# Second FFN of a decoder layer: units of mixed and plain chunks in turn, half-size raw buffers, output tiles turned over DRAM

## The chip, the cores and the metric

The kernel runs on one core of a Trainium2 chip. The metric is the device time of one execution in microseconds (us), as the median of several runs. The engines are TensorE (PE in the profile; its weight loads are PEld), VectorE (DVE), ScalarE (ACT), GpSimd (POOL) and SyncE (SP), which issues the weight transfers.

## What is computed

One layer of a decoder trunk on 256 positions (plus 16 meta tokens ahead of them), width 2048, in float32:

```
h = h + 0.5 * swiglu(rms_norm(h, g1), w_gate1, w_up1, w_down1)          # first FFN
z = rms_norm(h, g_mix) @ w_in                                           # attention, short convolution
h = h + (sigmoid(ga) * y_attn + sigmoid(gc) * y_conv) @ w_out           # output projection
h = h + 0.5 * swiglu(rms_norm(h, g2), w_gate2, w_up2, w_down2)          # second FFN, inner width 5632
return h[:, 16:]                                                        # the meta tokens are dropped

swiglu(x, g, u, d) = (silu(x @ g) * (x @ u)) @ d
```

The change lies in the second FFN and in the end of the output projection that feeds it. There the 256 positions are two tiles of 128 (j = 1, 2).

## The kernel before

**Numbers.** Each float32 operand is split into two float32r parts, `hi` and `lo`, and each product is three matmuls (`trio`, L360: x_hi w_hi, x_hi w_lo, x_lo w_hi). Activations are split once. Weights are split as they stream in: ScalarE copies the raw weight to `whi` (L129), VectorE subtracts to get `wlo` (L130).

**The stream of weights.** `Stream` (L71) is one list of raw loads and one list of *units*. A load is 2048 columns of 128 rows (1 MB), taken by SP into one of three buffers (`RAW_BUFS`). A unit is what is split at once, up to 1024 columns, two blocks of 512. `next` hands units to TensorE's code in order. When it turns to a unit it first runs the steps that are due in the queue `first` (put there by `early`), then splits the unit three ahead (`AHEAD`), then runs the due steps of the queue `waiting` (put there by `later`, with a lag in units; lag 1 is the very next unit). This fixes each engine's program order: all engines take their instructions in that order, and `split_pool` holds the parts of four units, so the split of a unit waits until TensorE has left the unit four earlier.

**Second FFN (`ffn_tokens`, L568).** The inner width is done in two groups of 6 and 5 *passes* (`GROUPS`). A pass (f) makes 512 gate columns and 512 up columns for both position tiles: 8 *chunks* of 256 input rows, each holding four 128 x 512 weight blocks. After the passes of a group come the down projections, in two halves (d = 0, 2) of two 512-column output tiles each, with 12 or 10 chunks.

A *plain* chunk is two units of four products: 8 products, 24 matmuls. A *mixed* chunk is a 2 x 2 x 2 block product by Strassen's method in Winograd's form: 7 products, 21 matmuls, in the four units a, b, c, d (2, 2, 2, 1 products). It asks VectorE for four sums of weight blocks (`part`, L138: t3 and b12 with a; t2 and t4 with b) and once per chunk place for sums of activations (`combos`, L585: four adds and a split into `comb` or `below`). In a pass the chunks `MIXED` (3 and 5) are mixed (in pass 0 of the first group only 5); in the down projections those in `DOWN_MIXED`.

**PSUM.** A pass uses all eight banks: four direct sums c[j, q] in the tiles `three` (two banks), `one` and `two`, and four sums m[1], m[5], m[6], m[7] of the mixed products in a second such set (`banks`, L667). The two sets change places from pass to pass: the next pass's direct sums go where this pass's mixed sums were, so these must be read out first. That is `spread` (L621): ScalarE copies m[1], then four VectorE adds combine m[6], m[7], m[5], m[5] into `u`. `gather` (L628) adds the direct sums and applies Silu on ScalarE, `times` (L636) multiplies gate and up.

**What follows a pass.** The product must be turned so that the inner dimension lies on the partitions. Between passes two large VectorE transposes of 32 x 32 blocks (`turn_blocks`, L643) are followed by five POOL transfers that move the blocks over DRAM (`move_blocks`, L652: one out, four back), and `split_blocks` splits into `mid`. After a group's last pass sixteen small transposes (`turn_columns`, L559) do it on VectorE alone. `down_combos` makes the activation sums of a mixed down chunk, 18 units after the pass that made its input.

**End of the output projection.** For each of four output tiles g, `add_out` (L1236) adds to the residual and sums squares, `turn_columns` turns the tile with sixteen small transposes between the next splits, and `to_act` (L1247) scales by the norm's gain and splits into `act`.

Of the kernel before, what the change touches and what calls it, by code (L numbers as in the profile page):

```python
# [65 lines left out]
MIXED = 3, 5  # L66
DOWN_MIXED = {6: (4, 6, 8), 5: (4, 7)}
RAW = 2048


class Stream:  # L71
# [14 lines left out]

    def add_mixed(self, src):

        g = len(self.loads)
        self.loads.append((src, RAW, ()))  # L90
        self.subs += [(g, part, 0, HALF) for part in "abcd"]

    def add(self, src, n, width, cuts=()):

        per = min(SUB // width, SUB // P)
        g = len(self.loads)
        self.loads.append((src, n * width, cuts))
        at = [0, *cuts, n] if cuts else [*range(0, n, per), n]
        for a, b in zip(at, at[1:]):
            self.subs.append((g, a * width, b - a, width))  # L100

    def load(self, upto, between=(), queues=()):
        between, queues = list(between), list(queues)
        while self.n_loaded < min(upto, len(self.loads)):
            src, n, cuts = self.loads[self.n_loaded]
            raw = self.raw_pool.tile([P, RAW], F32, name="raw")
            at = [0, *(c * P for c in cuts), n]
            for a, b in zip(at, at[1:]):
                (queues.pop(0) if queues else self.nc.sync).dma_start(raw[:, a:b], src[:, a:b])
                if between:  # L110
                    between.pop(0)()
            self.raw[self.n_loaded] = raw
            self.n_loaded += 1

    def split(self, upto):
        nc = self.nc
        while self.n_split < min(upto, len(self.subs)):
            g, c, kk, width = self.subs[self.n_split]
            self.load(g + RAW_BUFS)
            n = kk * width  # L120
            if n:
                raw = self.raw[g][:, c : c + n]
            else:
                raw = self.part(self.raw[g], c)
                n = raw.shape[1]
                kk = n // width
# [8 lines left out]
            if self.n_split == len(self.subs) or self.subs[self.n_split][0] > g or c == "b":  # L135
                self.load(g + 1 + RAW_BUFS)

    def part(self, raw, name):  # L138

        sub, add = self.nc.vector.tensor_sub, self.nc.vector.tensor_add  # L140
        b11, b12, b22, b21 = (raw[:, i * HALF : (i + 1) * HALF] for i in range(4))
        t3, t2, t4 = (self.mix[:, i * HALF : (i + 1) * HALF] for i in range(3))
        if name == "a":
            sub(t3, b22, b12)
            sub(b12, b12, b11)
            return raw[:, 2 * HALF :]
        if name == "b":
            add(t2, t3, b11)
            sub(t4, b21, t2)
            return raw[:, : 2 * HALF]  # L150
# [40 lines left out]
def tile_decoder_layer(  # L191
# [50 lines left out]
    gu = down = 0  # L242
    for n in GROUPS:
        for i in range(gu, gu + 8 * n):
            if i % 8 in MIXED[i < 8 :]:
                st.add_mixed(wgu2[i])
            else:
                st.add(wgu2[i], 4, 512)
        for pair in range(2):
            for i in range(2 * n):  # L250
                if i in DOWN_MIXED[n]:
                    st.add_mixed(wd2[down])
                else:
                    st.add(wd2[down], 4, 512)
                down += 1
        gu += 8 * n
# [9 lines left out]
    ssq = [const.tile([P, T], F32, name=f"ssq{i}") for i in range(2)]  # L266
    R = const.tile([P, T], F32, name="R")
    R2 = const.tile([P, T], F32, name="R2")
# [96 lines left out]
    def quads(c, m, x, mixed, n, after_mixed, tail=False):  # L365
# [4 lines left out]
        plan = []  # L370
        for i in range(n):
            k = 2 * i
            if i in mixed:
                s = [None, *(lambda part, q=q, i=i: mixed[i](q, part) for q in range(4))]
                plan.append([
                    [(c[1, 1], s[4], 0), (c[1, 0], of(k + 1, 1), 1)],
                    [(m[1], of(k, 1), 0), (m[5], s[1], 1)],
                    [(m[7], s[3], 0), (m[6], s[2], 1)],
# [13 lines left out]
        for i, units in enumerate(plan):  # L392
# [6 lines left out]
            if i == max(mixed):  # L399
                after_mixed()  # L400
# [998 lines left out]
```

## Time and profile before

| | us |
|---|---|
| median of 3 runs (2130.96 to 2131.1) | 2131.1 |
| the profiled execution, its own time | 2130.72 |
| its span, first to last instruction | 2129.0 |
| first matmul of the second FFN, from the span's start | 1419.12 |
| last matmul | 2124.10 |
| TensorE busy | 2118.0 (99%) |
| VectorE busy | 1489.5 (70%) |
| ScalarE busy | 1015.7 (48%) |
| granted TensorE clock, mean over the span | 1.0 of full speed |

A row of the timeline gives start (us from the span's start), length (us), engine, line, operation, output<-input and, behind x, how many like it follow each other; in square brackets stands how long the engine was idle ahead of it and what ended that. Matmuls are pipelined: their shown lengths (0.39 us) overlap, so it is the distance between starts that tells whether TensorE was held up. Rows of the order, in fences of their own, show in which order an engine's instructions stand; they hold no times.

### The profile page before, as it was taken

What the parts mean: (1) busy time and instruction counts of PE and PEld (TensorE: products, weight loads), DVE (VectorE), ACT (ScalarE), POOL (GpSimd) and SP (SyncE); (2) the same over time, 40 slices, a digit from 0 to 9 for tenths busy, and PEclk for the clock granted to TensorE, in tenths of its full rate; (3) what the DMA queues carried; (4) which work ended last, traced back from release to release, by engine and by line L of the source; (5) the groups of instructions that cost most, each with busy time, mean ns of one, the idle gap of its engine ahead of it and who ended that gap; (6) DMA issues with size and microseconds to landing.
All of it is one profiled execution on the core that took longest, in us unless ns stands there. A gap on an engine that the chain in (4) does not pass through costs nothing.

```text
span 2129.0 us, 31231 instructions
## 1 busy us (share of the span) xinstructions
PE 2118.0 (99%) x12809; PEld 1903.5 (89%) x12809; DVE 1489.5 (70%) x1991; ACT 1015.7 (48%) x1271; POOL 34.7 (2%) x73
## 2 busy tenths in 40 slices
PE   9999999999999999999999999999999999999999
PEld 9999999999999998799988888887888788888877
DVE  7555544455555556677677477898889988888896
ACT  6444433344444445455544444445555555455543
POOL 0000000000000000000000000000000000000000
PEclk9999999999999999999999999999999999999999
DMA  7555555555545555444455555555666565566654
GB/s 265 187 179 179 177 179 178 177 179 179 179 177 180 178 174 177 171 163 166 160 190 197 197 181 198 195 181 198 233 220 226 190 215 200 204 228 231 220 185 155
DMA packets 59935, 407.04 MB, mean 191 GB/s; under 512 B 7056, under 2 KB 7824, under 8 KB 12432
## 3 DMA queue, kind: packets, MB, share of 16 engines
q1 hardware_dynamic: 55872, 393.51, 53.2%
q0 software_dynamic: 3344, 10.49, 1.5%
q8 instruction: 100, 1.64, 0.3%
q10 hardware_dynamic: 576, 1.05, 0.1%
q14 instruction: 43, 0.35, 0.0%
HBM read 398.20 MB, written 6.82 MB: 190 GB/s over the span
## 4 chain that ended last, share of the span: by engine, by line
PE 94%; DVE 4%; issue 1%; ACT 1%; DMA 1%; ACTq 0%; DVEq 0%
PE three L362 5%; PE three L363 5%; PE three L361 5%; PE pd L329 4%; PE pd L327 4%; PE pd L328 4%; PE pg L328 4%; PE pu L328 4%; PE pu L329 4%; PE pg L329 4%; PE pg L327 4%; PE pu L327 4%; PE pgt L357 3%; PE pgt L356 3%; PE pgt L355 3%; PE one L362 2%
## 5 line engine op out<-in xcount | busy, mean ns | idle before, releaser
L130 DVE TENSOR_TENSOR wlo<-raw,whi 128x1024 fp32r<-128x1024 f32 (+1 forms) x749 | 908.5, 1219 | 589.0 <-ACT whi L129 583.9
L129 ACT ACTIVATE whi<-raw 128x1024 fp32r<-128x1024 f32 (+1 forms) x749 | 784.9, 1054 | 899.3 <-PE pd L328 146.3
L328 PE MATMUL pd<-mid,whi 128*128 128x272 f32 x704 | 201.8, 287 | 0.0
L329 PE MATMUL pd<-mid,wlo 128*128 128x272 f32 x704 | 201.8, 287 | 0.0
L327 PE MATMUL pd<-mid,whi 128*128 128x272 f32 x704 | 201.8, 287 | 0.0
L327 PE MATMUL pu<-act,whi 128*128 128x272 f32 x672 | 192.7, 287 | 0.0
L328 PE MATMUL pg<-act,whi 128*128 128x272 f32 x672 | 192.6, 287 | 0.0
L327 PE MATMUL pg<-act,whi 128*128 128x272 f32 x672 | 192.6, 287 | 0.0
L328 PE MATMUL pu<-act,whi 128*128 128x272 f32 x672 | 192.6, 287 | 0.0
L329 PE MATMUL pu<-act,wlo 128*128 128x272 f32 x672 | 192.6, 287 | 0.0
L329 PE MATMUL pg<-act,wlo 128*128 128x272 f32 x672 | 192.6, 287 | 0.0
L327 PEld LDWEIGHTS pd<-mid,whi 128*128 128x128 f32 x704 | 132.7, 188 | 0.0
L329 PEld LDWEIGHTS pd<-mid,wlo 128*128 128x128 f32 x704 | 132.7, 188 | 0.0
L328 PEld LDWEIGHTS pd<-mid,whi 128*128 128x128 f32 x704 | 132.6, 188 | 0.0
L362 PE MATMUL three<-wlo,act 128*128 128x512 f32 x331 | 129.1, 390 | 1.1 <-DVE wlo L130 1.1
L363 PE MATMUL three<-whi,act 128*128 128x512 f32 x331 | 128.8, 389 | 0.0
L361 PE MATMUL three<-whi,act 128*128 128x512 f32 x331 | 128.8, 389 | 0.0
L327 PEld LDWEIGHTS pg<-act,whi 128*128 128x128 f32 x672 | 126.6, 188 | 0.0
L328 PEld LDWEIGHTS pu<-act,whi 128*128 128x128 f32 x672 | 126.6, 188 | 0.0
L329 PEld LDWEIGHTS pu<-act,wlo 128*128 128x128 f32 x672 | 126.6, 188 | 0.0
L327 PEld LDWEIGHTS pu<-act,whi 128*128 128x128 f32 x672 | 126.6, 188 | 0.0
L328 PEld LDWEIGHTS pg<-act,whi 128*128 128x128 f32 x672 | 126.6, 188 | 0.0
(330 smaller groups left out, 4327.2 us busy)
## 6 DMA issues: line engine op xcount, KB each, us to landing
raw<-in_wgu_dram SPq DMA_DIRECT2D x174, 1024.0 KB, 4.8
raw<-in_wd_dram SPq DMA_DIRECT2D x88, 1024.0 KB, 4.8
raw<-in_wcv_dram SPq DMA_DIRECT2D x24, 1024.0 KB, 4.8
raw<-in_wgc_dram SPq DMA_DIRECT2D x24, 1024.0 KB, 4.8
raw<-in_wga_dram SPq DMA_DIRECT2D x24, 1024.0 KB, 4.8
raw<-in_wo_dram SPq DMA_DIRECT2D x16, 1024.0 KB, 4.9
raw<-in_wqi_dram SPq DMA_DIRECT2D x8, 1024.0 KB, 4.8
raw<-in_wq_dram SPq DMA_DIRECT2D x8, 1024.0 KB, 4.8
```

The costliest lines, as they stand in the source:

```text
L129: nc.scalar.activation(hi[:, :n], raw, AF.Copy)
L130: nc.vector.tensor_sub(lo[:, :n], raw, hi[:, :n].bitcast(F32))
L327: nc.tensor.matmul(ps, whi, xhi, start=first, stop=False)
L328: nc.tensor.matmul(ps, whi, xlo, start=False, stop=False)
L329: nc.tensor.matmul(ps, wlo, xhi, start=False, stop=last)
L355: nc.tensor.matmul(ps, xhi, whi, start=k + i == 0, stop=False)
L356: nc.tensor.matmul(ps, xhi, wlo, start=False, stop=False)
L357: nc.tensor.matmul(ps, xlo, whi, start=False, stop=k + i == n - 1)
L361: nc.tensor.matmul(ps, x(0), w[0], start=first, stop=False)
L362: nc.tensor.matmul(ps, x(0), w[1], start=False, stop=False)
L363: nc.tensor.matmul(ps, x(1), w[0], start=False, stop=last)
```

## The change

1. **Taking turns** (`order`, new). A mixed chunk followed by a plain one becomes a, plain 0, b, c, plain 1, d, where a, b, c, d stood together and the plain units after them. The mixed places move: `MIXED` from 3 and 5 to 2 and 5 (pass 0 of the first group keeps 5 alone), `DOWN_MIXED` from 4, 6, 8 and 4, 7 to 5, 7, 9 and 5, 7. The number of mixed chunks is the same, so the matmuls are as many. The four products of a plain unit and the two of a mixed one stand in another order, and the weights are laid out to match.
2. **Half-size raw buffers.** In the second FFN a load is 1024 columns (512 KB), into halves of the same three buffers. A plain unit is one load; a mixed chunk holds two from a until b.
3. **Output tiles over DRAM.** In the output projection `turn_columns` gives way to `turn_out`, two large transposes, and `move_blocks`; `to_act` reads the blocks where they lie, with 8 VectorE steps of 128 x 128 for 4 of 128 x 256, two units later than before.
4. **When steps are due.** `spread` and `gather` are put in by `early`, ahead of the split, no longer by `later`. `times` moves from lag 2 to 3 (2 stays after a group's last pass), the turning from 3 to 5, the moving from 4 to 6, `split_blocks` from 13 to 14; the adds of a down half's `u` come one unit sooner; the norm's root moves from lags 8 to 10 to 3 to 5. `down_combos` keeps its lag of 18. `act_combos` runs at lag 6 for chunk 5, as before, and at 16 for chunk 2 (18 for chunk 3 before), and puts one of the four sums into `act` in place.
5. **Names and parts not used.** The norm's four rows share one tile `few`, which also takes the place of `gather`'s tile `s`. A way to make the weight sums ahead of time (`job`, `MADE`) is added with `MADE` empty, so it issues nothing.

```diff
-MIXED = 3, 5
-DOWN_MIXED = {6: (4, 6, 8), 5: (4, 7)}
+MIXED = 2, 5
+FIRST_MIXED = 5,
+MADE = ()
+DOWN_MIXED = {6: (5, 7, 9), 5: (5, 7)}
...
+def order(n, mixed, made=()):
+    out, i = [], 0
+    while i < n:
+        if i not in mixed:
+            out += [(i, "0"), (i, "1")]
+        else:
+            a, b, c, d = [(i, x) for x in ("ABCD" if i in made else "abcd")]
+            if i + 1 in mixed or i + 1 == n:
+                out += [a, b, c, d]
+            else:
+                i += 1
+                out += [a, (i, "0"), b, c, (i, "1"), d]
+        i += 1
+    return out
...
+    def load_one(self, between=(), queues=()):
+        src, n, cuts, slots = self.loads[self.n_loaded]
+        if slots == 1:
+            tile, half = divmod(self.n_ring, 2)
+            if tile < RAW_BUFS and not half:
+                self.ring.append(self.raw_pool.tile([P, RAW], F32, name="raw"))
+            raw = self.ring[tile % RAW_BUFS][:, half * SUB : half * SUB + SUB]
+            self.n_ring += 1
...
+    def fill(self):
+        while self.n_loaded < len(self.loads) and (
+            sum(x[3] for x in self.loads[self.kept : self.n_loaded + 1]) <= 2 * RAW_BUFS
+        ):
+            self.load_one()
...
+    def move_blocks(x):
+        hold = scratch.tile([P, 4, 2, P], F32, name="hold", bufs=2)
+        nc.gpsimd.dma_start(hold, x)
+        of_quarter = hold.rearrange("(r f) q j c -> q f r (j c)", r=4)
+        for q in range(4):
+            nc.gpsimd.dma_start(x[q * 32 : q * 32 + 32], of_quarter[q])
...
-                        st.later(lambda: act_combos(1), 6)
-                        st.later(lambda: act_combos(0), 18)
-                    now = {i: mixed[i] for i in MIXED[f == g == 0 :]}
-                    quads(c, m, act_tokens, now, 8, lambda m=m: st.later(lambda: spread(m)))
-                    st.later(lambda x=x, c=c, box=box: gather(x, c, box))
-                    st.later(lambda box=box: times(box), 2)
+                        rest = [i for i in MIXED if i not in FIRST_MIXED]
+                        for i, lag in zip((*FIRST_MIXED, *rest), (6, 16, 17)):
+                            st.later(lambda i=i: act_combos(i), lag)
+                    now = {i: mixed[i] for i in (MIXED if f or g else FIRST_MIXED)}
+                    quads(c, m, act_tokens, now, 8, lambda m=m: st.early(lambda: spread(m)), made=MADE)
+                    st.early(lambda x=x, c=c, box=box: gather(x, c, box))
...
-                        st.later(lambda box=box: turn_blocks(box), 3)
-                        st.later(lambda box=box: move_blocks(box["x"]), 4)
-                        st.later(lambda to=to, box=box: split_blocks(to, box["x"]), 13)
+                        st.later(lambda box=box: times(box), 3)
+                        st.later(lambda box=box: turn_gated(box), 5)
+                        st.later(lambda box=box: move_blocks(box["x"]), 6)
+                        st.later(lambda to=to, box=box: split_blocks(to, box["x"]), 14)
                         for q, i in enumerate(i for i in DOWN_MIXED[n] if i // 2 == f):
                             st.later(lambda i=i, n=n: down_combos(DOWN_MIXED[n].index(i), i), 18 + q)
...
                     def after(m=m, d=d):
-                        st.later(lambda: spread(m))
-                        st.later(lambda: half_to(ht[d], u[:, :2]), 2)
-                        st.later(lambda: half_to(ht[d + 1], u[:, 2:]), 3)
+                        st.early(lambda: spread(m))
+                        st.later(lambda: half_to(ht[d], u[:, :2]))
+                        st.later(lambda: half_to(ht[d + 1], u[:, 2:]), 2)
...
-            for r in range(4):
-                st.later(lambda g=g, r=r, box=box: turn_columns(box["m"], ht[g], r), 2 + r)
-            st.later(lambda g=g, box=box: to_act(g, box["m"]), 6)
+            st.later(lambda g=g, box=box: turn_out(g, box), 2)
+            st.later(lambda box=box: move_blocks(box["x"]), 3)
+            st.later(lambda g=g, box=box: to_act(g, box["x"]), 8)
```

More of the change, by code (lines that the diff above doesn't have):

```diff
@@ L102, in load @@
     def load(self, upto, between=(), queues=()):
         between, queues = list(between), list(queues)
[L104 to L113, printed above, removed]
+        while self.n_loaded < upto:
+            self.load_one(between, queues)
@@ L242, in tile_decoder_layer @@
     gu = down = 0
+    made = []
+    scratch = ctx.enter_context(tc.tile_pool(name="scratch", bufs=1, space=bass.MemoryType.DRAM))
     for n in GROUPS:
[L244 to L256, printed above, removed]
+        for f in range(n):
+            now = MIXED if gu else FIRST_MIXED
+            sums = {i: scratch.tile([P, RAW], F32, name=f"made{gu + i}") for i in now if i in MADE}
+            made += [(gu + i, x) for i, x in sums.items()]
+            for i, name in order(8, now, MADE):
+                st.add_part(name, wgu2[gu + i], sums.get(i))
+            gu += 8
+        for _ in range(2):
+            for i, name in order(2 * n, DOWN_MIXED[n]):
+                st.add_part(name, wd2[down + i])
+            down += 2 * n
     const.tile([P, 16], F32, name="lead")
@@ L390, in quads @@
+            plan.append((unit, i == max(mixed) and name in "dD"))
+        flat = [id(p[0]) for unit, _ in plan for p in unit]
         at = 0
         blocks = []
-        for i, units in enumerate(plan):
-            for unit in units:
-                blocks = blocks + [st.next()] + st.rest()
-                for ps, xx, b in unit:
-                    trio(ps, xx, blocks[b], id(ps) not in flat[:at], id(ps) not in flat[at + 1 :])
-                    at += 1
-                blocks = [] if unit else blocks
-            if i == max(mixed):
+        for unit, last in plan:
+            blocks = blocks + [st.next()] + st.rest()
+            for ps, xx, b in unit:
+                trio(ps, xx, blocks[b], id(ps) not in flat[:at], id(ps) not in flat[at + 1 :])
+                at += 1
+            blocks = [] if unit else blocks
+            if last:
@@ L576, in ffn_tokens @@
             u = fp.tile([P, 4, 512], F32, name="u")
[L577 to L578 removed]
+            comb = fp.tile([P, len(MIXED), 3, 2, P], F32R, name="comb")
+            mixed = {
+                i: lambda q, part, n=n, i=i: comb[:, n, q - 1, part] if q else halves[:, 2 * i, part, 1]
+                for n, i in enumerate(MIXED)
+            }
             late["junk"] = lambda: u[:, 0]
```

187 lines of the change are left out of this document (110 added, 77 removed).

## The prediction

> **What bounds the kernel now.** I read the page first, then TensorE's waits, then the timeline at the places these named. By the page's busy row
>
> ```profile
> PE 2118.0 (99%) x12809; PEld 1903.5 (89%) x12809; DVE 1489.5 (70%) x1991; ACT 1015.7 (48%) x1271; POOL 34.7 (2%) x73
> ```
>
> TensorE has no idle time worth the name, but a matmul's shown end is modelled, so only its starts count. TensorE's timeline in the second FFN: the first matmul, the last, the first of passes 2 and 5 of the first group (passes count from 0), then the two ends of three disturbed stretches (with two more matmuls of the second).
>
> ```profile
> 1419.12 0.39 PE L361 MATMUL three<-whi,act 128*128 128x512 f32 x1
> 1507.76 0.39 PE L361 MATMUL three<-whi,act 128*128 128x512 f32 x1
> 1634.24 0.39 PE L361 MATMUL three<-whi,act 128*128 128x512 f32 x1
> 2124.10 0.39 PE L363 MATMUL two<-whi,mid 128*128 128x512 f32 x1
> 1443.60 0.39 PE L361 MATMUL one<-whi,act 128*128 128x512 f32 x1
> 1457.44 0.39 PE L361 MATMUL one<-whi,act 128*128 128x512 f32 x1
> 1695.44 0.39 PE L361 MATMUL one<-whi,mid 128*128 128x512 f32 x1
> 1695.83 0.50 PE L362 MATMUL one<-wlo,mid 128*128 128x512 f32 x1
> 1696.17 0.40 PE L363 MATMUL one<-whi,mid 128*128 128x512 f32 x1
> 1703.16 0.39 PE L361 MATMUL two<-whi,below 128*128 128x512 f32 x1
> 2035.00 0.39 PE L361 MATMUL one<-whi,mid 128*128 128x512 f32 x1
> 2042.72 0.39 PE L361 MATMUL two<-whi,below 128*128 128x512 f32 x1
> ```
>
> A pass has 6 plain chunks of 24 matmuls and 2 mixed ones of 21, 186 in all; three passes take 1634.24 - 1507.76 = 126.48 us, so a matmul takes 0.2267 us. The stage has 3075 of them (11 x 186, 3 more in pass 0, which has one mixed chunk only, and 44 down chunks, 34 x 24 + 10 x 21). From the first start to the last are 704.98 us, and 3074 x 0.2267 = 696.8: TensorE loses **8.2 us** here. It loses them at three places: 13.84 us for 45 matmuls (10.20) in pass 0, and twice 7.72 us for 24 matmuls (5.44) as the down projections begin: 3.64 + 2.28 + 2.28 = 8.20. Nothing else is lost in this stage, so 8.2 us is all that the change can win; the matmuls stay as many.
>
> Why they are lost shows VectorE at the second place:
>
> ```profile
> 1686.07 3.57 DVE L470 STREAM_TRANSPOSE mt<-s 32x256 f32<-32x256 f32 x8
> 1689.68 1.23 DVE L130 TENSOR_TENSOR wlo<-raw,whi 128x1024 fp32r<-128x1024 f32 x1
> 1690.93 3.59 DVE L470 STREAM_TRANSPOSE mt<-s 32x256 f32<-32x256 f32 x8
> 1694.55 1.23 DVE L130 TENSOR_TENSOR wlo<-raw,whi 128x1024 fp32r<-128x1024 f32 x1
> ```
>
> Sixteen transposes stand between splits, and a wlo that ends at 1694.55 + 1.23 = 1695.78 holds the matmul that should follow 1695.44 by 0.23 us: it starts at 1695.83, 0.05 after the wlo, and the one behind it 0.34 later, 0.11 over the pitch. So what counts is VectorE's backlog, unit by unit.
>
> **The change part by part.** I measure from T, the start of the first matmul after the last mixed chunk of a pass. A plain unit is 12 matmuls, 2.72 us; mixed units are 1.36, 1.36, 1.36 and 0.68. VectorE and ScalarE at the end of pass 4 before:
>
> ```profile
> 1601.76 1.30 DVE L647 STREAM_TRANSPOSE mt<-s 128x512 f32<-128x512 f32 x2
> 1602.98 0.65 DVE L144 TENSOR_TENSOR mix<-raw 128x512 f32<-128x512 f32 x1
> 1607.87 1.22 DVE L130 TENSOR_TENSOR wlo<-mix,whi 128x1024 fp32r<-128x1024 f32 x1
> 1611.11 2.54 DVE L130 TENSOR_TENSOR wlo<-raw,whi 128x1024 fp32r<-128x1024 f32 x2 [1.09 <-ACT whi L129]
> 1626.25 0.69 DVE L623 TENSOR_TENSOR u<-one,u 128x512 f32<-128x512 f32 x1
> 1628.31 0.68 DVE L626 TENSOR_TENSOR u<-three,u 128x512 f32<-128x512 f32 x1
> 1628.90 1.22 DVE L130 TENSOR_TENSOR wlo<-raw,whi 128x1024 fp32r<-128x1024 f32 x1
> 1630.04 0.69 DVE L589 TENSOR_TENSOR mix<-mid 128x512 f32<-128x512 f32 x1
> 1632.37 0.56 DVE L422 TENSOR_TENSOR below<-mix,below 128x384 fp32r<-128x384 f32 x1 [0.39 <-ACT below L421]
> 1636.74 1.22 DVE L630 TENSOR_TENSOR s<-three,u 128x1024 f32<-128x1024 f32 x1
> 1640.31 1.23 DVE L130 TENSOR_TENSOR wlo<-raw,whi 128x1024 fp32r<-128x1024 f32 x1 [1.16 <-ACT whi L129]
> 1641.46 1.41 DVE L639 SCALAR_TENSOR_TENSOR s<-u,rcol,s 128x512 f32<-128x512 f32 x2
> 1642.78 1.22 DVE L130 TENSOR_TENSOR wlo<-raw,whi 128x1024 fp32r<-128x1024 f32 x1
> ```
>
> ```profile
> 1612.48 0.39 PE L361 MATMUL three<-whi,act 128*128 128x512 f32 x1
> ```
>
> ```profile
> 1610.01 1.06 ACT L129 ACTIVATE whi<-raw 128x1024 fp32r<-128x1024 f32 x1 [0.73 <-PE three L363]
> 1612.68 1.06 ACT L129 ACTIVATE whi<-raw 128x1024 fp32r<-128x1024 f32 x1 [0.30 <-PE one L363]
> ```
>
> Starts give the pitches. A whi starts 0.20 us after TensorE has left the unit four earlier (1612.48 to 1612.68), its wlo 1.10 later (1610.01 to 1611.11), the next VectorE step 1.14 after that; the four adds of spread take 2.65 to the next step and end at 2.74; the combos end after 2.89 and give way to the next step 0.08 sooner, as a wlo does (1628.90 + 1.22 against 1630.04), after 2.81; gather to the next wlo is 3.57 (Silu on ScalarE between); times 1.32; the two large transposes 1.22; a mixed chunk's parts a to c 4.89 + 1.14 = 6.03.
>
> *Taking turns.* Before, a, b, c, d stand together: 4.76 us of TensorE for 6.03 of VectorE and part d besides. Now two plain units (5.44 and 2.28) lie between. In mid-pass the starts above show nothing lost before, and VectorE gets more room: 0.
>
> *Spread and combos.* On VectorE at the end of pass 4 of the first group (L623 to L626 are spread, L589 to L422 the combos, L630 gather) stood before
>
> ```order
> L623 TENSOR_TENSOR u<-one,u 128x512
> L624 TENSOR_TENSOR u<-two,u 128x512
> L625 TENSOR_TENSOR u<-three,u 128x512
> L626 TENSOR_TENSOR u<-three,u 128x512
> L130 TENSOR_TENSOR wlo<-raw,whi 128x1024
> L589 TENSOR_TENSOR mix<-mid 128x512
> ...
> L422 TENSOR_TENSOR below<-mix,below 128x3x128
> L130 TENSOR_TENSOR wlo<-raw,whi 128x1024 x3
> L630 TENSOR_TENSOR s<-three,u 128x1024
> ```
>
> and on the same engine at the same place (now L711 to L714, L677 to L466, L718) stand
>
> ```order
> L177 TENSOR_TENSOR wlo<-raw,whi 128x1024 x3
> L677 TENSOR_TENSOR mix<-mid 128x512
> ...
> L466 TENSOR_TENSOR below<-mix,below 128x3x128
> L711 TENSOR_TENSOR u<-one,u 128x512
> L712 TENSOR_TENSOR u<-two,u 128x512
> L713 TENSOR_TENSOR u<-three,u 128x512
> L714 TENSOR_TENSOR u<-three,u 128x512
> L177 TENSOR_TENSOR wlo<-raw,whi 128x1024 x2
> L718 TENSOR_TENSOR few<-three,u 128x1024
> ```
>
> The combos have gone ahead of spread, and spread has lost two of its four units of lead: chunk 5's last part now has only chunk 7 behind it. The next pass's first two products need spread's PSUM tiles: TensorE's wait on `one` is for its first add, that on `three` for its last. The wlo ahead of the combos waits, through its whi, for the last unit but one: whi at T - 0.68 + 0.20 = T - 0.48, wlo T + 0.62, combos T + 1.76, spread T + 4.57 to T + 7.31. TensorE wants `three` at T + 5.44 + 0.68 = T + 6.12: late by 1.19, with the 0.05 and 0.11 of the stall above **1.35**. All of VectorE follows late: gather at 4.57 + 2.65 + 2 x 1.14 = 9.50, wlo 13.07, and with wlo 1.14, a to c 6.03, wlo 1.14, times 1.32, transposes 1.22, the wlo for unit 3-1 ends at 13.07 + 10.85 + 1.22 = 25.14. From T, six plain units, 3-0 and three mixed ones lie ahead of it: 7 x 2.72 + 3 x 1.36 = 23.12, and its second matmul is due at 23.12 + 0.23 + 1.35 = 24.70: 0.44 + 0.16 = **0.60** more. So 1.95 for a pass end with combos. The order shows six such: pass 0 (act_combos for chunk 2), passes 3, 4, 5 of the first group, 3 and 4 of the second. Without combos all is 2.81 earlier: spread ends at 4.50, the wlo at 22.33 against 23.35; these pass ends cost nothing.
>
> *Before a down projection* the wlo at 13.07 is followed by wlo, times, wlo, eight transposes (1686.07 to 1689.68, 3.61), wlo 1.25, eight more (3.62), and the wlo of unit 3-1, which ends at 13.07 + 1.14 + 1.14 + 1.32 + 1.14 + 3.61 + 1.25 + 3.62 + 1.23 = 27.52; nine plain units lie ahead (24.48), so it is due at 24.48 + 0.23 + 1.35 = 26.06: 1.46 + 0.16 = 1.62, in all 2.97. The first mixed chunk (now 5, not 4) leaves two more plain units to recover in, so no stall follows there, but the sum is above the old 2.28. Between the two halves of a down projection no combos stand: 0. At the end of the kernel spread's 2.74 and two adds of a wlo's length (1.14 each) end inside the last 24 matmuls (5.44): 0.
>
> *Output tiles over DRAM.* VectorE in the last output tile before, and now, with the next pass's splits between:
>
> ```order
> L130 TENSOR_TENSOR wlo<-raw,whi 128x1024
> L470 STREAM_TRANSPOSE mt<-first 32x2x4x32 x4
> L130 TENSOR_TENSOR wlo<-raw,whi 128x1024
> L470 STREAM_TRANSPOSE mt<-first 32x2x4x32 x4
> L130 TENSOR_TENSOR wlo<-raw,whi 128x1024
> L1253 SCALAR_TENSOR_TENSOR act<-mt,small,act 128x256 x4
> L589 TENSOR_TENSOR mix<-act 128x512
> ```
>
> ```order
> L177 TENSOR_TENSOR wlo<-raw,whi 128x1024
> L637 STREAM_TRANSPOSE mt<-first 128x4x4x32 x2
> L177 TENSOR_TENSOR wlo<-raw,whi 128x1024
> L702 TENSOR_TENSOR sums<-sums 128x2 x2
> L703 TENSOR_TENSOR sums<-sums 128x2
> L177 TENSOR_TENSOR wlo<-raw,whi 128x1024
> ```
>
> Sixteen small transposes (twice the 3.6 above: 7.2) become two (1.22): 6 us leave VectorE ahead of the first mixed chunk, which lost 3.64. I put that place at 0; if half of the relief fails, 1. The DMAs wait on POOL, whose rows are
>
> ```profile
> hold<-mt POOLq DMA_DIRECT2D x9, 512.0 KB, 4.8
> mt<-hold POOLq DMA_DIRECT2D x36, 128.0 KB, 5.0
> raw<-in_wgu_dram SPq DMA_DIRECT2D x174, 1024.0 KB, 4.8
> raw<-in_wkw_dram SPq DMA_DIRECT2D x1, 640.0 KB, 3.8
> ```
>
> 4.8 + 5.0 and five issues, and to_act comes six units (16 us) after the transposes. Covered: 0; a late one would hold the whi behind it on ScalarE.
>
> *Half loads.* SP issues 264 loads of 512 KB for 132 of 1 MB, in one queue, each behind the VectorE step that frees its half. TensorE takes one per 704.98 / 264 = 2.67 us. Loads overlap:
>
> ```profile
> 1397.42 0.33 SPq L109 DMA_DIRECT2D raw<-in_wo_dram  x1
> 1399.97 35.56 SPq L109 DMA_DIRECT2D raw<-in_wgu_dram  x7
> ```
>
> The second was issued 2.55 us after one that takes 4.8. So 3.8 us each (the 640 KB row, the nearest) is hidden: 0, at most 0.5 us a pass if the three that wait for part b come late. The Trainium skill, "DMA: Bandwidth & Descriptors", section "Bandwidth", asks for DMAs of at least 1 MiB; by its fit (section "Anatomy of one DMA") of 2.0 us and 436 GB/s a full load is 4.4 us, where the row has 4.8, and a half load 3.2 us (estimate); without overlap that would cost 264 x 0.5 = 140 us. No trace here shows half loads yet.
>
> The spare parts (`MADE` empty, `few`, `early` for gather, the norm's root five units sooner) move under 1 us of VectorE each: 0. **Sum:** lost after 4 x 1.95 + 2 x 2.97 = 13.7, lost before 8.2: **+5.5 us**. The profiled run took 2130.7 us (span 2129.0) and becomes 2136.2; the median of the three runs, 2131.1, stands 0.4 above it and becomes 2136.6.
>
> **The rivals.**
> *Absorbed:* the combos run early enough that spread ends before T + 6.1. For it: VectorE sat idle 1.16 and 1.09 in the rows above. Against: that idle time is spent waiting for whi, and whi for TensorE. Point: combos at T + 0.5, not T + 1.76. Then only the 8.2 us go: **2122.9**, faster. 0.11.
> *First wait only:* TensorE's 1.35 comes six times, but later steps catch up (0.5 us of slack decides): 8.1 lost, 8.2 won: **2131.0**, no change. 0.19.
> *Loads:* half loads one at a time at 3.8 us: 264 x (3.8 - 2.67) = 298 us more, **2429**. Against: the two issues 2.55 us apart. 0.02. The rule of the Trainium skill above speaks for this one, with its smaller price.
>
> **How the numbers follow.** Forecast 0.68. Less than 0.2%, 4.3 us, cannot be told from no change here. Range: low where stalls of 1.2 us come six times and the rest is won (2130), high where five more pass ends lose 0.9 and the first place 1 (2142). Faster: the first rival, 0.11. Same: the second, and 0.02 of the forecast at its low end, 0.21. Slower: the forecast's other 0.66 and the loads, 0.68.
>
> **What would show it.** Right: TensorE's starts jump by about 1.35 us at the second product of passes 1, 4, 5 and the first down unit, `three` waiting for L714, and again at unit 3-1 for L177; nothing between 1419 and 1460. Wrong: matmuls evenly 0.2267 us apart across pass ends, or SP loads as releasers.

## The result, and the profile after

The changed kernel takes 2142.9 us (median of 4 runs, 2138.9 to 2143.6) where the kernel before takes 2131.0 (4 runs beside it): ratio 1.0052, 95% interval 1.0034 to 1.0069, 11.8 us slower. The forecast was 2136.6, with 2142 as the upper end of its range: the sign was right, but the loss is more than twice the 5.5 us that were forecast. The shortest of the four runs has a mean granted TensorE clock of 1.000, the other three 0.999.

TensorE's timeline in the second FFN of the kernel after, as it was shown of before: the first and the last matmul, the start of pass 1, unit 6-0 of pass 0 and two matmuls from the middle of that unit. (Unit 6-0 is plain unit 0 of chunk 6, unit 5a part a of the mixed chunk 5.)

```profile
1419.18 0.39 PE L409 MATMUL one<-whi,act 128*128 128x512 f32 x1
2136.55 0.39 PE L411 MATMUL two<-whi,mid 128*128 128x512 f32 x1
1467.52 0.40 PE L409 MATMUL one<-whi,act 128*128 128x512 f32 x1
1467.98 0.40 PE L411 MATMUL one<-whi,act 128*128 128x512 f32 x1
1469.54 0.47 PE L409 MATMUL three<-whi,act 128*128 128x512 f32 x1 [1.16 <-DVE u L714]
1449.06 0.39 PE L411 MATMUL three<-whi,act 128*128 128x512 f32 x1
1450.47 0.50 PE L409 MATMUL one<-whi,act 128*128 128x512 f32 x1 [1.02 <-ACT whi L176]
1451.73 0.50 PE L410 MATMUL one<-wlo,act 128*128 128x512 f32 x1 [0.76 <-DVE wlo L177]
1453.52 0.63 PE L409 MATMUL two<-whi,act 128*128 128x512 f32 x1
1453.94 0.63 PE L410 MATMUL two<-wlo,act 128*128 128x512 f32 x1
```

From first to last start are 717.37 us, and the matmuls need 696.8 as before: 20.6 us are lost where 8.2 were. The difference, 12.4, is nearly the whole change of the profiled run, 12.9 (2143.6 against 2130.7). I split the loss by unit: the distance from one unit's first matmul to the next unit's, less 0.2267 us for each matmul. Pass 4's first unit starts at 1597.08 and the next at 1601.24, so it loses 4.16 - 2.72 = 1.44.

| lost at | forecast, us | measured, us |
|---|---|---|
| first unit of a pass behind combos (passes 1, 4, 5; 4 of the second group) | 4 x 1.35 | 1.42, 1.44, 1.44, 1.43 |
| unit 3-1 of these passes | 4 x 0.60 | 0.57, 0.56, 0.55, 0.58 |
| first unit of the two down projections | 2 x 1.35 | 1.43, 1.42 |
| unit 3-1 there | 2 x 1.62 | 1.58, 1.58 |
| pass 0: units 1-1, 2-0, 5a, 6-0 | 0 | 0.38, 1.16, 1.19, 2.74 |
| pass 1: 5d, 7-0 | 0 | 0.39, 0.70 |
| sum | 13.7 | 14.0 + 6.6 = 20.6 |

TensorE's waits over the stage name both halves: `three` six times for spread's last add, and, in the last row, `whi`, which the forecast's sum had nowhere.

```profile
PE three L409 <- DVE u L714: 6.9, 6, 1.2
PE one L410 <- DVE wlo L177: 5.4, 9, 1.3
PE one L409 <- ACT whi L176: 1.2, 2, 1.0
```

VectorE at the end of pass 3, the place worked out beforehand (here T = 1591.64): the split ahead of the combos, their first and last step, spread, gather, the wlo behind it, the transposes, the wlo of unit 3-1.

```profile
1592.25 1.23 DVE L177 TENSOR_TENSOR wlo<-raw,whi 128x1024 fp32r<-128x1024 f32 x1 [1.49 <-ACT whi L176]
1593.39 0.68 DVE L677 TENSOR_TENSOR mix<-mid 128x512 f32<-128x512 f32 x1
1595.73 0.56 DVE L466 TENSOR_TENSOR below<-mix,below 128x384 fp32r<-128x384 f32 x1 [0.39 <-ACT below L465]
1596.22 0.69 DVE L711 TENSOR_TENSOR u<-one,u 128x512 f32<-128x512 f32 x1
1598.28 0.68 DVE L714 TENSOR_TENSOR u<-three,u 128x512 f32<-128x512 f32 x1
1601.14 1.22 DVE L718 TENSOR_TENSOR few<-three,u 128x1024 f32<-128x1024 f32 x1
1604.71 1.23 DVE L177 TENSOR_TENSOR wlo<-raw,whi 128x1024 fp32r<-128x1024 f32 x1 [1.16 <-ACT whi L176]
1614.38 1.30 DVE L637 STREAM_TRANSPOSE mt<-few 128x512 f32<-128x512 f32 x2
1615.60 1.18 DVE L177 TENSOR_TENSOR wlo<-raw,whi 128x1024 fp32r<-128x1024 f32 x1
```

Spread was put at T + 4.57 to T + 7.31, that is 1596.21 to 1598.95; it stands at 1596.22 to 1598.96. Gather was put at 1601.14, the wlo behind it at 1604.71, the end of the wlo of 3-1 at 1616.78: each is there to 0.01 us. This half of the argument held.

The other half is on ScalarE. Its timeline, with what it waited for, and POOL's transfers at the same time; the third output tile is `mx`, the fourth `mt` (L1335 is to_act; L465 is the split that split_blocks uses, here of pass 0's product, run in pass 1):

```profile
1416.66 1.06 ACT L176 ACTIVATE whi<-raw 128x1024 fp32r<-128x1024 f32 x1 [1.66 <-PE po L405]
1423.36 1.71 ACT L1335 ACTIVATE act<-mx,small 128x256 fp32r<-128x256 f32 x4 [5.64 <-DMA mx<-hold]
1424.97 1.05 ACT L176 ACTIVATE whi<-raw 128x1024 fp32r<-128x1024 f32 x1
1429.34 2.94 ACT L176 ACTIVATE whi<-raw 128x1024 fp32r<-128x1024 f32 x3
1447.76 1.71 ACT L1335 ACTIVATE act<-mt,small 128x256 fp32r<-128x256 f32 x4 [3.67 <-DMA mt<-hold]
1449.37 1.04 ACT L176 ACTIVATE whi<-raw 128x1024 fp32r<-128x1024 f32 x1
1503.43 1.16 ACT L465 ACTIVATE mid<-mt 128x512 fp32r<-128x512 f32 x2 [4.73 <-DMA mt<-hold]
```

```profile
1408.68 0.56 POOL L645 DMA_DIRECT2D hold<-mx  x1 [16.28 <-DVE mx L637]
1412.66 2.19 POOL L648 DMA_DIRECT2D mx<-hold  x4 [3.42 <-ACT whi L176]
1433.15 0.56 POOL L645 DMA_DIRECT2D hold<-mt  x1 [18.30 <-DVE mt L637]
1441.17 2.18 POOL L648 DMA_DIRECT2D mt<-hold  x4 [7.46 <-DMA hold<-mt]
```

The fourth tile leaves at 1433.15, is out at 1441.17 (8.0 us for the write) and is read by to_act at 1447.76: a trip of 14.6 us. ScalarE came to that step at 1447.76 - 3.67 = 1444.09, and everything behind it waited, the next whi first: it starts at 1449.37, and its matmul, due 0.23 after 1449.06, at 1450.47.

Waiting is not all of unit 6-0's 2.74 us. For the stretch from 1452.30 to 1455.80 the profile shows, for TensorE alone (stretch, its length, busy time and matmuls, granted clock, the DMA engines' busy share, GB/s):

```profile
1452.30:1455.80 3.50, 3.50 (x10) 0.51 0.24 22
```

The granted clock is half there, and the matmuls start 0.43 us apart (1453.52 to 1453.94) and not 0.23. This costs 1.6 us, so pass 0 loses 3.9 us by waits and 1.6 by the clock. The kernel before has no such stretch in this stage. It begins 0.6 us after a matmul that had waited; what sets it off is not shown (e1 below has longer waits and no such stretch).

The transfers of after, with the median time from issue to landing in us:

```profile
raw<-in_wgu_dram SPq DMA_DIRECT2D x177, 512.0 KB, 5.0
raw<-in_wd_dram SPq DMA_DIRECT2D x88, 512.0 KB, 4.7
hold<-mt POOLq DMA_DIRECT2D x10, 512.0 KB, 6.0
mx<-hold POOLq DMA_DIRECT2D x12, 128.0 KB, 7.2
```

A half load takes 4.7 to 5.0 us in the median, as long as a full one (4.8); they overlap, so the rival of 2429 us is out. The estimate of 3.2 us, from the fit of the Trainium skill ("DMA: Bandwidth & Descriptors", "Anatomy of one DMA"), which that section gives for the GpSimd path, is near the fastest half load of this stage (3.4 us), not the median. The write of a turned tile went from 4.8 to 6.0 us.

### The profile page after: what moved, and what is told of

Read it like the earlier page. It is cut to its first block, busy times and chain, and to the rows that moved or that the text cites. A ratio compares the mean times of both kernels' runs of the same rounds, so it can differ in the third digit from the quotient of the medians.

```text
span 2141.8 us, 31599 instructions
## 1 busy us (share of the span) xinstructions
PE 2121.6 (99%) x12809; PEld 1903.6 (89%) x12809; DVE 1468.5 (69%) x1953; ACT 1013.4 (47%) x1273; POOL 45.7 (2%) x93
## 4 chain that ended last, share of the span: by engine, by line
PE 90%; DVE 5%; DMA 2%; issue 1%; ACT 1%; POOL 0%; SPq 0%; DVEq 0%; ACTq 0%
PE three L409 4%; PE three L410 4%; PE three L411 4%; PE pd L375 4%; PE pd L377 4%; PE pd L376 4%; PE pu L377 4%; PE pg L377 4%; PE pg L376 4%; PE pu L376 4%; PE pu L375 4%; PE pg L375 4%; PE pgt L404 3%; PE pgt L405 3%; PE pgt L403 3%; PE one L410 2%
## 5 line engine op out<-in xcount | busy, mean ns | idle before, releaser
L409 PE MATMUL three<-whi,act 128*128 128x512 f32 x352 | 137.7, 391 | 4.6 <-DVE u L714 4.6
L410 PE MATMUL three<-wlo,act 128*128 128x512 f32 x352 | 137.6, 391 | 0.1
L411 PE MATMUL three<-whi,act 128*128 128x512 f32 x352 | 137.3, 390 | 0.0
L375 PEld LDWEIGHTS pu<-act,whi 128*128 128x128 f32 x672 | 126.6, 188 | 0.0
L377 PEld LDWEIGHTS pg<-act,wlo 128*128 128x128 f32 x672 | 126.5, 188 | 0.0
```

Of the source, the lines that this page charges most:

```text
L375: nc.tensor.matmul(ps, whi, xhi, start=first, stop=False)
L377: nc.tensor.matmul(ps, wlo, xhi, start=False, stop=last)
L409: nc.tensor.matmul(ps, x(0), w[0], start=first, stop=False)
L410: nc.tensor.matmul(ps, x(0), w[1], start=False, stop=False)
L411: nc.tensor.matmul(ps, x(1), w[0], start=False, stop=last)
```

## The experiments

Two theories on the missed 6.6 us. Mine: the turn over DRAM takes some 15 us by itself, and ScalarE, in order, hands its lateness on. The rival: half loads are the root. For the 14.0 at the pass ends: VectorE's backlog, as forecast, against the place of spread alone. Ratios are to the kernel before on the same chip, with 95% intervals; "pass 0, 1" leaves out what belongs to pass ends (first units and 3-1; for e5 also 1-1 and 2b of the passes behind combos).

| run | median us | ratio (interval) | profiled us | lost in pass 0, 1 | at pass ends | elsewhere |
|---|---|---|---|---|---|---|
| after | 2142.9 | 1.0052 (1.0034 to 1.0069) | 2143.6 | 6.6 | 14.0 | 0 |
| e1 | 2140.3 | 1.0047 (1.0031 to 1.0064) | 2140.2 | 3.2 | 14.0 | 0 |
| e2 | 2139.5 | 1.0040 (1.0025 to 1.0055) | 2139.9 | 0 | 14.0 | 2.3 |
| e3 | 2131.3 | 1.0004 (0.9995 to 1.0014) | 2131.3 | 3.3 | 0 | 4.6 |
| e4 | 2137.7 | 1.0031 (1.0018 to 1.0044) | 2136.3 | 5.9 | 2.2 | 5.4 |
| e5 | 2145.9 | 1.0072 (1.0057 to 1.0087) | 2149.4 | 6.7 | 19.9 | 0 |
| e6 | 2135.0 | 1.0023 (1.0013 to 1.0032) | 2131.0 | 2.2 | 5.9 | 0 |
| e7 | 2142.5 | 1.0055 (1.0040 to 1.0070) | 2140.9 | 4.1 | 14.1 | 0 |
| e8 | 2139.6 | 1.0041 (1.0026 to 1.0056) | 2140.0 | 5.7 | 10.8 | 0 |
| e9 | 2138.8 | 1.0037 (1.0023 to 1.0051) | 2140.0 | 3.0 | 14.0 | 0.2 |
| e10 | 2138.1 | 1.0033 (1.0021 to 1.0046) | 2137.8 | 0 | 14.1 | 0.2 |
| e11 | 2128.6 | 0.9989 (0.9980 to 0.9998) | 2128.6 | 1.4 | 3.4 | 0.7 |
| e12 | 2130.9 | 1.0004 (0.9996 to 1.0013) | 2133.6 | 6.0 | 3.9 | 0.4 |
| e13 | 2138.4 | 1.0036 (1.0023 to 1.0050) | 2137.8 | 0.9 | 14.0 | 0 |
| e14 | 2128.5 | 0.9990 (0.9981 to 0.9999) | 2128.5 | 0.6 | 4.4 | 0 |
| e15 | 2127.2 | 0.9985 (0.9976 to 0.9994) | 2126.4 | 0 | 3.3 | 0.2 |

In every row the profiled time less its three losses is 2122.5 to 2123.6 us (before: 2130.7 - 8.2 = 2122.5). So these losses account for the differences to within 1.1 us. Some of them are clock, as at 6-0 in after: of the losses in pass 0, 1.6 us in e4 and 2.9 in e12, and at each down projection of e5 1.6 us, fall in stretches of half the granted clock. Each of these begins within 1.4 us behind a matmul that had waited. The runs of most of these kernels scatter more (0.9 to 9 us from the lowest to the highest) than those of the kernel before (1.2 to 1.8), and a profile is one of them: e6's lies 4 us under its median.

### Pass 0 and 1

**e1: output tiles turned on VectorE again.**

```diff
...
-            st.later(lambda g=g, box=box: turn_out(g, box), 2)
-            st.later(lambda box=box: move_blocks(box["x"]), 3)
-            st.later(lambda g=g, box=box: to_act(g, box["x"]), 8)
+            for r in range(4):
+                st.later(lambda g=g, r=r, box=box: turn_columns(box["m"], ht[g], r), 2 + r)
+            st.later(lambda g=g, box=box: to_act(g, box["m"]), 6)
```

> The output tiles are turned by sixteen small transposes on VectorE again; everything else as after. Theory (ScalarE, in order, is held behind to_act, which waits for the turn over DRAM): the 5.5 us lost in pass 0 fall to about the 3.6 of the kernel before, the 14.0 at the pass ends and the 1.1 in pass 1 stay: about 2141.0, 1.8 less than after. Rival (the half loads hold up pass 0): the 5.5 stay, 2142.9.

2140.3. Pass 0 loses 3.2, near the 3.64 of before; the pass ends are what they were; pass 1 loses nothing in this run. So the turn over DRAM is a part of the cause. How large a part e1 does not say: the sixteen transposes bring VectorE's backlog back, and of the 2.3 us less in pass 0, 1.6 are the half clock of after, which this profile does not have.

**e2: whole loads again.**

```diff
-            self.loads.append((x, x.shape[1], (), 1))
+            self.loads.append((x, x.shape[1], (), x.shape[1] // SUB))
...
+            if name == "0":
+                self.plain = load(src)
+            g, at = self.plain, SUB * int(name)
+            self.subs.append((lambda: self.raw[g][:, at : at + SUB], 2, HALF, (g,) if at else ()))
...
-                self.pair = load(src[:, :SUB]), load(src[:, SUB:])
+                self.pair = load(src)
```

> One load of 2048 columns for each chunk again; order, pass ends and the turn over DRAM as after. Theory (the turn over DRAM takes about 15 us by itself): pass 0 and 1 still lose about 6.6 us, 2142.9. Rival (the bunched half loads slow the turn's transfers): the transfers fall to the 4.8 and 5.0 us of before, the 6.6 go, about 2136.3.

Passes 0 and 1 lose nothing: my theory fell here, the turn by itself is not too long. POOL at the fourth tile, and ScalarE in pass 4:

```profile
1430.45 0.56 POOL L643 DMA_DIRECT2D hold<-mt  x1 [15.96 <-DVE mt L635]
1433.93 2.18 POOL L646 DMA_DIRECT2D mt<-hold  x4 [2.92 <-DMA hold<-mt]
```

```profile
1618.59 2.01 ACT L174 ACTIVATE whi<-raw 128x1024 fp32r<-128x1024 f32 x2 [4.81 <-DMA raw<-in_wgu_dram]
```

The write takes 3.5 us instead of 8.0, and to_act finds its tile after 12.5 us instead of 14.6. The second row shows what half loads are good for: with whole buffers and units taking turns, the load ahead of unit 6-0 keeps ScalarE waiting 4.8 us, and that unit loses 0.9, 0.9 and 0.5 us in three passes, 2.3 in all. So the time fell by 3.3 us only.

**e3: the kernel before, with its output tiles over DRAM** (`turn_out`, `move_blocks` and the new `to_act` put into it; no other edit).

> The kernel before with its output tiles turned over DRAM and nothing else changed. Theory (the turn over DRAM holds ScalarE whatever the loads are): the place in pass 0 loses about 5.5 us instead of 3.6, 2132.9 against 2131.0. Rival (only together with half loads is it late): that place loses 0 to 1, 2127.4 to 2128.4.

No change: 2131.3, ratio 1.0004. The place in pass 0 loses 3.3, between the two forecasts: to_act waits 4.3 us there, as against 1.5 in e2. The loss falls on 5b to 6-0; that chunk 5's units stand together in this kernel and leave no room to absorb the wait is my reading, not tried by itself. Six microseconds of VectorE work less ahead of that place win 0.3 us.

**e7 and e13: the waiting steps later.** e7 moved split_blocks alone; to_act stayed at 8, against what its expectation says. e13 moves both.

```diff
-            st.later(lambda g=g, box=box: to_act(g, box["x"]), 8)
+            st.later(lambda g=g, box=box: to_act(g, box["x"]), 9)      # e13 only
-                        st.later(lambda to=to, box=box: split_blocks(to, box["x"]), 14)
+                        st.later(lambda to=to, box=box: split_blocks(to, box["x"]), 15)
```

> to_act one unit later (lag 9 for 8) and split_blocks one unit later (15 for 14): what waits for DRAM stands one whi further back on ScalarE. Theory (ScalarE held behind these waits): the 1.5 us at units 1-1 and 2-0 and the 1.1 in pass 1 go, unit 6-0, which needs the last output tile itself, still loses about 3: about 2140. Rival (the loads are what is late): no change, 2142.9.

> After, with to_act and split_blocks both one unit later (lags 9 and 15 for 8 and 14). Theory (ScalarE in order hands the late transfer on): the wait for the third output tile shrinks from 5.6 to about 2.9 us and the 1.5 lost at units 1-1 and 2-0 go, the 1.1 of pass 1 go, about 3 stay at units 5a and 6-0, where the last tile is itself needed: 2139.8. Rival (the losses there have another cause): as after or as the run with only split_blocks later, 2142.5.

e7: 2142.5; pass 1 loses nothing, pass 0 still 4.1 (in after, without the half clock, 3.9). e13: 2138.4, and pass 0 loses nothing at all, not even at 6-0, where I had left 3. Its ScalarE rows for the third and fourth tile:

```profile
1422.22 1.71 ACT L1335 ACTIVATE act<-mx,small 128x256 fp32r<-128x256 f32 x4 [1.99 <-DMA mx<-hold]
1444.59 1.71 ACT L1335 ACTIVATE act<-mt,small 128x256 fp32r<-128x256 f32 x4 [1.86 <-DMA mt<-hold]
```

The fourth trip is nearly as long as in after (1430.84 to 1444.59, 13.8 us), but ScalarE has one more whi done before it waits, and waits 2.0 and 1.9 us instead of 5.6 and 3.7; what TensorE has in hand covers that. With nothing lost at the third tile, the fourth starts 2.3 us sooner too. This shows the hand-over on ScalarE: nearly the same transfers, one unit more of work ahead of the wait, and the 3.9 us of waits go, and with them the 1.6 of half clock behind them. Pass 1 is less clear: e13 loses 0.9 us there, at 7-0, with split_blocks at the lag at which e7 lost nothing.

**e9 and e10: what of half loads makes the turn long.** e9 issues each whole load as two of 1024 columns into the same buffer; e10 has whole loads in pass 0 only.

```diff
# e9, on top of e2
-            self.loads.append((x, x.shape[1], (), x.shape[1] // SUB))
+            self.loads.append((x, RAW, (SUB // P,), 2))
# e10, on top of after
-                st.add_part(name, wgu2[gu + i], sums.get(i))
+                st.add_part(name, wgu2[gu + i], sums.get(i), gu == 0)
```

> As the kernel with one load of 2048 columns a chunk, but each load is issued as two of 1024 columns one behind the other into the same buffer, so that sizes are those of after and the times of issue those of whole loads. If the size of the loads lengthens the write to DRAM in pass 0: it takes 6 to 8 us, pass 0 and 1 lose 5.5 to 6.6 us and the time is 2145 to 2146 (the 2.3 lost at unit 6-0 with whole buffers stay). If their times of issue do (half a buffer that is free earlier starts a load beside the write): the write takes 3.5 to 4.4, pass 0 loses nothing, 2139.5.

> After, with one load of 2048 columns a chunk in pass 0 alone and half loads from pass 1 on. Theory (half loads beside the turn over DRAM cost pass 0 and 1 their 6.6 us): those two lose 0 to 1, the pass ends 14.0 as in after: 2136.3 to 2137.4. Rival (the loss of pass 0 comes of the half loads in general, or of chance): 2142.9.

| | read of the third tile, us | write of the fourth, us | its whole trip, us |
|---|---|---|---|
| after (half loads, half a buffer at a time) | 10.7 | 8.0 | 14.6 |
| e4 (the same) | 10.2 | 7.1 | 14.8 |
| e9 (half loads, issued when a whole buffer is free) | 10.4 | 3.5 | 12.4 |
| e2, e10 (whole loads) | 8.3, 8.0 | 3.5, 3.5 | 12.5, 12.4 |

Read: from the issue of the four transfers back to to_act's start, which waited for them in each. Neither theory of e9 is the whole answer. This *write* is long where loads are issued as halves come free and short where they wait for whole buffers, whatever their size. The *read* of the third tile is some 2 us longer with 512 KB loads, whenever issued (that of the fourth is not: 6.6 us in after, 9.0 in e2), and e9 loses 2.2 us at units 1-1 and 2-0 for it (3.0 in all). e10, with whole loads in pass 0 alone, loses nothing there: 2138.1, 0.7 over its forecast. So the loss in pass 0 needs both parts of the change: the turn with whole loads costs 0 (e2, e10), half loads without the turn 3.2 (e1) where before lost 3.6, both together 5.5, 1.6 of them by the clock.

What was found of the write is no rule for other places: in e4, with halves issued as they come free, the nine writes between passes land after 3.1 to 3.4 us. What these and the short ones above share is that hardly any load was under way when they were issued: none in e2, e9 and e10, one with at most 0.8 us to go in e4's nine, but one with 2.0 to go in after (issued at 1431.67, landed at 1435.15). In all traces together, the 58 writes at whose issue no load had more than 0.9 us to go land after 3.1 to 3.8 us, and the 107 with three half loads under way after 5.5 to 7.9; between these the order is not clean. So what is under way at the write's issue is a rival to the times of issue of the loads, and no run separates the two.

Why these transfers hinder each other stays open: in the 10 us around the long write the DMA engines are less busy in after than in e2.

```profile
1430.00:1440.00 10.00, 9.03 (x39) 7.06 (x39) 8.19 (x17) 5.67 (x7) 0.56 (x1) 1.00 0.71 228
```

```profile
1430.00:1440.00 10.00, 10.00 (x46) 8.29 (x45) 8.14 (x21) 4.32 (x7) 2.74 (x5) 1.00 0.85 284
```

(After, then e2; the last two columns are the DMA engines' busy share and GB/s.)

### The pass ends

**e4: the units of a mixed chunk stand together.** `order` gives a, b, c, d for every mixed chunk.

> The units of a mixed chunk stand together again, all else as after. VectorE ledger: four units lie behind the last mixed part instead of two and spread comes ahead of the combos, so the 1.35 to 1.44 at the first product of a pass and the 0.57 at unit 3-1 go; about 1.4 each stay where a down projection begins, and 4 to 6.6 us in passes 0 and 1: 2129 to 2132. Rival (the pass ends are held by the half loads, not by the place of spread): about 2143.

2137.7, above the forecast 2129 to 2132. As expected the losses at first units and at 3-1 of the passes are gone and 1.1 each stay at the down projections; passes 0 and 1 lose 5.9, 1.6 of them by the clock (half from 1453.3 to 1456.7). What I missed are 5.4 us in chunk 2, at 2b to 3-0 of the three passes behind combos: spread, gather and the chunk's sums meet there, one chunk sooner than in the kernel before, where the first mixed chunk is 3.

**e5: combos one unit later** (`(6, 16, 17)` becomes `(6, 17, 18)`, `18 + q` becomes `19 + q`).

> The combos of the next chunks are registered one unit later (lags 19 and 17 for 18 and 16), so that spread stands ahead of them on VectorE. VectorE ledger (the sum of the work ahead of unit 3-1 counts, not its order): the 1.4 at the first product of a pass goes, unit 3-1 loses about 1.95 in its place (2.97 before a down projection): no change, 2142.9. Rival (spread behind the combos is what costs): six times 1.35 go for good, 2134.8.

2145.9, 3 us over after. The rival is out: with spread first nothing is won. But my ledger failed too: not the same loss in another place, but 2.45 instead of 2.0 in each of four passes and 5.0 instead of 3.0 at each down projection. (1.6 of each 5.0 are half clock, from 1710.0 to 1713.5 and from 2054.8 to 2058.2; the waits come to 3.4.) ScalarE at the end of pass 3:

```profile
1598.56 0.31 ACT L465 ACTIVATE mid<-mix 128x128 fp32r<-128x128 f32 x1 [4.57 <-DVE mix L678]
1599.29 0.53 ACT L465 ACTIVATE below<-mix 128x384 fp32r<-128x384 f32 x1 [0.42 <-DVE mix L681]
1599.72 1.04 ACT L176 ACTIVATE whi<-raw 128x1024 fp32r<-128x1024 f32 x1
```

The next whi now stands behind the combos' splits, VectorE waits for it, and the wlo behind gather starts at 1605.51. T is 1591.98 in this run, so that is T + 13.53, 0.46 later than in after (T + 13.07), while TensorE has not lost its 1.35 and wants it sooner: unit 1-1 loses 1.1, before 3-1 is reached.

**e6: combos two units earlier** (`(6, 14, 15)`, `16 + q`).

> The combos are registered two units earlier (lag 16 for 18, 14 for 16). VectorE ledger: they fall where VectorE waits for whi, spread ends at about T + 5.5 and TensorE wants it at T + 6.1, the rest follows 1.8 us earlier: of the 14.0 lost at pass ends about 2.8 stay, 2131.7. Rival (there is no idle time to fill, the stall moves into the mixed chunk ahead): 2142.9.

TensorE's waits:

```profile
PE one L410 <- DVE wlo L177: 4.5, 8, 1.3
PE three L410 <- DVE wlo L177: 0.3, 1, 0.3
```

The wait on `three` for spread is gone: the first units lose 0.10 instead of 1.4. Unit 3-1 keeps its 0.55 (and 1.6 at the down projections): VectorE's later steps come 1.35 us sooner (the wlo behind gather at T + 11.72, T + 13.07 in after), not the 1.8 expected, and TensorE comes 1.3 us sooner too. Median 2135.0, 7.9 less than after; of the 14.0, 8.1 are gone in the profile, where I had said 11.2.

**e8: the last pass of a group over DRAM** (`times`, `turn_gated`, `move_blocks`, `split_blocks` at lags 2, 3, 4, 14 in place of `turn_columns`).

> The last pass of a group is turned over DRAM as the others are, so the sixteen small transposes (7.2 us of VectorE) ahead of unit 3-1 of the down projection become two large ones (1.2). VectorE ledger: the two losses of 1.58 at that unit go, the 1.43 at its first product stay: 2139.7. Rival (split_blocks holds ScalarE there as in passes 0 and 1): 1 to 3 us lost in their place, no change or up to 3 more.

2139.6, as forecast: both losses of 1.58 at unit 3-1 of the down projections are gone, and the eight transposes twice ahead of it (first row, after) are two large ones (second row, e8).

```profile
1697.75 3.58 DVE L514 STREAM_TRANSPOSE mt<-few 32x256 f32<-32x256 f32 x8
```

```profile
1697.33 1.30 DVE L637 STREAM_TRANSPOSE mt<-few 128x512 f32<-128x512 f32 x2
```

### Versions that put this together

**e11:** e10's whole loads in pass 0, e6's lags, e8's last pass. **e12:** e1's columns instead of the whole loads, else the same.

> Three corrections together: whole loads in pass 0, combos two units earlier, the last pass of a group turned over DRAM. Ledger: 0.10 at each first product of a pass, 0.56 at unit 3-1 of four passes, nothing at the down projections, 0 to 1 in passes 0 and 1: 2.8 to 3.8 lost, 2125.6 to 2126.6, under both kernels. Rival (the losses of passes 0 and 1 only move on): 2.2 to 6 more, 2128 to 2132.

> Output tiles turned by small transposes again, half loads everywhere, combos two units earlier, the last pass of a group turned over DRAM. Ledger: 3.2 lost in pass 0 and 2.8 at the pass ends: 2128.8. Rival (what is saved at the pass ends is lost again in the mixed chunks): 2132 or more.

e11 takes 2128.6, under both kernels (by 14 us and, ratio 0.9989, 2.2 us); 2 to 3 over its forecast: 1.4 in pass 1, where the first turn meets half loads, and 1.3 around pass 5. e12 takes 2130.9, no different from before: 6.0 lost in pass 0, 2.8 more than in e1. TensorE's waits there are those of e1 (1.8 and 0.8 us, in e1 1.9 and 0.8); the difference is the clock, in the columns of the row shown of after:

```profile
1446.40:1453.30 6.90, 6.14 (x15) 0.51 0.25 76
```

The half clock costs 2.9 us here.

**e14:** e11 with split_blocks at lag 15. **e15:** e11 with whole loads in passes 0 and 1 (`gu < 16`).

> The version with three corrections, and split_blocks one unit later (15 for 14). Theory: the 1.4 lost at parts 5d and 7-0 of pass 1, where split_blocks waits for DRAM, go: 2127.2. Rival (the wait only holds the next whi instead, or the combos behind it): 2128.6 or more.

> The version with three corrections, and whole loads in passes 0 and 1. Theory (the write to DRAM in pass 1 takes 8.5 us beside half loads): it takes 3.5 to 4.5, the 1.4 go: 2127.2. Rival (a whole buffer comes free later, and the load behind it is late for unit 6-0): 0.5 to 0.9 lost there, 2128.

e14 does not differ from e11 (2128.5): pass 1 loses 0.6 instead of 1.4, the first units 0.37 instead of 0.10. e15 has the lowest median: 2127.2, as forecast, ratio 0.9985 (0.9976 to 0.9994); its interval overlaps those of e11 and e14. Its write in pass 1, and split_blocks, which no longer waits:

```profile
1479.42 0.56 POOL L656 DMA_DIRECT2D hold<-mt  x1 [44.58 <-DVE mt L648]
1483.66 2.18 POOL L659 DMA_DIRECT2D mt<-hold  x4 [3.68 <-DMA hold<-mt]
```

```profile
1493.13 1.13 ACT L476 ACTIVATE mid<-mt 128x512 fp32r<-128x512 f32 x2
```

## Why the prediction was right and wrong

*Taking turns, mid-pass 0:* right in after, where no unit inside a later pass loses anything. e4 shows that it is not free of effect, though: without it, with the first mixed chunk at place 2, 5.4 us are lost in chunk 2.

*Spread and combos, 1.35 + 0.60 at four pass ends; 1.35 + 1.62 at two:* right, 14.0 for 13.7, the steps to 0.01 us. The same working was not good enough for two variants: it put e5 at no change (3 us over after; its profile has 1.6 us more of half clock than that of after) and e6 at 2.8 left (5.9). It followed VectorE alone, left out which whi stands behind which wait on ScalarE (e5), put VectorE's gain at 1.8 us where it was 1.35, and forgot that TensorE's next need comes sooner when an earlier stall goes (e6).

*Output tiles over DRAM, "Covered: 0; a late one would hold the whi behind it on ScalarE":* this is the step that failed, by 5.5 us in pass 0: 3.9 of waits and 1.6 of half clock behind them, for which the sum had no term (1.1 more in pass 1 by the same kind of wait, at split_blocks). The mechanism was named and given no price. Both sides of the comparison were off. The trip was taken as 4.8 + 5.0 and five issues, 4.8 + 5.0 + 0.56 + 2.18 = 12.5; e2 with its whole loads takes 12.5 too, but by luck: there the write lands after 3.2 us and the four reads after 6.0 to 7.3. In after the trip was 14.6: the durations came from a kernel without half loads. The cover was taken as six units, 16 us, as if ScalarE and VectorE kept TensorE's pace. They did not: ScalarE had waited 5.6 us for the third tile and 1.9 more ahead of the last tile's squares, so the whi of unit 2-0, ahead of the transposes, starts at 1429.34, where TensorE had left unit 0-0, four units earlier, at 1421.90. Of these 7 us ScalarE makes up some 4 before it comes to to_act. The transposes start at 1431.56

```profile
1431.56 1.30 DVE L637 STREAM_TRANSPOSE mt<-first 128x512 f32<-128x512 f32 x2
```

and ScalarE stood at to_act at 1444.09, 12.5 us later, 10.9 after the write's issue at 1433.15. So the trip of 14.6 us had a cover of 10.9. e13 shows that one unit more is enough for pass 0. "If half of the relief fails, 1" bounded the wrong thing: the relief on VectorE came, and a new wait took its place.

*Half loads, 0, at most 0.5 a pass:* right for the weights: TensorE lost nothing to waits for them in after, and e2 shows that they even save 2.3 us, but their effect on another queue's transfers was not looked for. Parts 2 and 3 were costed one by one at 0; e2 and e10 show that the turn costs nothing in pass 0 with whole loads, and e1 that half loads without it lose 3.2 there, under the 3.6 of before: the cost lies in the two together.

*The rivals:* Absorbed fell, but e6 shows its mechanism: combos two units earlier do free spread. First wait only fell: unit 3-1 lost its 0.56 in each pass. Loads fell. *What would show it:* the jumps came at the places named; "nothing between 1419 and 1460" was wrong.

*Open:* how loads and turned tiles hinder each other inside the queues, what sets off the stretches of half clock, and the scatter of e6 and e3 (8.8 and 6.9 us from the lowest run to the highest), of which each profile shows one run.

## What to carry to other kernels

An engine that works in order must be costed at the time at which it reaches a waiting step, not at the time at which the result is needed: the cover of a transfer is the distance in that engine's own program, from where a late engine starts the transfer to where it has caught up, and all that stands behind the wait pays. Two parts of a change that add nothing one by one can be dear together when they share a resource, here transfers; the durations of one must be taken under the load of the other, or bounded by it. A step moved out of a stall is not won until the next need of each engine has been followed as well. And a loss behind a stall is not all stall: the granted clock of the stretch belongs beside it.

## What was not expected of the hardware

In this stage a 512 KB load of 128 rows lands after 4.8 us in the median of after, a 1 MB load after 4.9 in before and 5.0 in e2: under the load of this stage the size did not show in the median, but in the fastest (3.4 us against 4.6). A 512 KB write to DRAM from another queue, that of the fourth output tile, took 3.5 to 3.8 us, up to the next issue, beside whole loads and 6.8 to 8.7 beside half loads started as halves of buffers came free, with the DMA engines 85% busy in e2 of the first kind and 71% in after; beside e4's half loads the writes between passes landed after 3.1 to 3.4 us. Four reads of 128 KB, those of the third tile, were there for to_act 7.2 to 8.5 us after the first was issued beside 1 MB loads and 9.1 to 10.9 beside 512 KB loads; for the fourth tile it is the other way, 8.9 to 9.4 and 5.6 to 8.9. Behind a stall TensorE's granted clock stood at half for 3.4 us in after, e4 and twice in e5, and for 6.8 us in e12, and behind an equal stall in e1 it did not.
